# Modulation blocks of a two-layer hybrid trunk: two per filler among the heads, four moved to the branch projections

## The chip, the cores and the metric

The kernel runs on one core of a Trainium2 chip, as one launch. The metric is the device time of one execution in microseconds. The core has engines with instruction streams of their own: TensorE (PE; its weight loads are PEld) multiplies, VectorE (DVE) and ScalarE (ACT) do elementwise work, GpSimd (POOL) some rare steps, and SyncE (SP) issues most of the DMA loads. Each engine runs its row in order; semaphores join the rows.

## The reference

Two layers (L0, L1) work on one sequence of 256 positions with 1024 channels, in float32. A conditioning vector `c` gives each layer six modulation vectors of 1024 channels: shift, scale and gate for the mixer (1) and for the feed-forward part (2).

```
c_act = silu(c)
for l in range(2):
    mod = c_act @ ada_w[l] + ada_b[l]                 # 6 x 1024
    sh1, sc1, g1, sh2, sc2, g2 = split(mod, 6)
    h = rmsnorm(x) * (1 + sc1) + sh1
    x = x + g1 * mixer(h)
    h = rmsnorm(x) * (1 + sc2) + sh2
    x = x + g2 * conv_ffn(h)
return rmsnorm(x)
```

The mixer projects `h` once and feeds two branches of eight heads each: an attention with low-rank q and kv (block-causal softmax), and an mLSTM (weights `exp` of gate differences times `q k`, a normaliser, a head norm). Then `merged = sigmoid(g_mla) * (y_mla @ w_br_mla) + sigmoid(g_mlstm) * (y_mlstm @ w_br_mlstm)`, and `merged @ w_out`.

## The kernel before

Activations lie with their channels on the 128 partitions, as eight blocks of 128 channels by 256 positions. Every float32 matmul is done as three products of rounded parts, `fm_steps`: weight high part by activation high part, high by low, low by high. The class `_Weights` loads each weight tile `raw` (128x1024, 512 KB, seven buffers) on SP's queue; ScalarE copies it to the rounded high part `whi` (five buffers) and VectorE subtracts to get the low part `wlo` (four buffers). The matmuls of a weight tile cannot run before both.

The order of the work is written out as units. A `unit` (L265) is a list of slots, each a group of TensorE matmuls (12 in a slot of what follows). Ahead of each slot it calls `advance()`, by which all side generators (evictions, heads, merges) issue their next step, then it issues one piece of the weight splitting, then, where the slot's number is in `ada`, one `pump()`, and then the slot's matmuls.

`pump` (L344) takes the next modulation block from `background` and issues `ada_block` (L337): a DMA of 512 KB on SP's queue into one of two `wada` buffers, and one VectorE `scalar_tensor_tensor` over 128x1024 that multiplies by `silu(c)` and sums each row into one column of `mod`. After the eighth block of a modulation vector a tiny addition of the bias follows (and a halving for g1). The order in `background` is g1, sc2, sh2, g2 of the layer, eight blocks each, and in layer 0 then the first vectors of layer 1. Blocks of g1 are needed where `x` is updated by the output projection; sc2 and sh2 (blocks 9 to 24) at `norm_columns` (L1109), behind the branch projections, where `while (l, 3) not in done: pump()` would pump what is missing.

Among the heads the units are fillers: `run_filler(i)` (L813) is one weight tile of the gate or value projections, four slots, and the two generators of a head (`mla_head` L839, `mlstm_head` L885) advance by one step at each slot. So an attention head's steps (scores, maxima, `exp`, `reciprocal` and scaling, transposes on TensorE, copy, product with v) lie between the slots. `fill()` (L1051) runs the ten late fillers 0, 1, 4 to 11: one ahead of the heads, one after each head but 1 and 3, and the rest behind the last. Behind them come the eight units of the branch projections, of two slots each: for each half `c` of the columns two of the attention branch (`merge_a`, into `ua`) and two of the mLSTM branch (`merge_b`, which ends in the merged high part `mh` on ScalarE and low part `ml` on VectorE). Then the output projection, in which layer 0 pumps five blocks (`OUT_PUMPS`) and layer 1 none.

VectorE, ScalarE and GpSimd instructions may be moved by the scheduler, but not ahead of the one issued eight (two on GpSimd) before on the same engine; and a block's instruction stays behind the VectorE instruction issued last before it. Both layers run the same code.

Of the kernel before, what the change touches and what calls it, by code (L numbers as in the profile page):

```python
# [57 lines left out]

FILLERS_3 = (4, 5, 6, 7)
OUT_PUMPS = ((1, 2, 3, 4, 5), ())
UP_PUMPS = ((4, 6, 8), ())
DOWN_PUMPS = ((2, 2, 2, 2, 2, 1, 1, 1, 1, 1, 1), (1,) * 8)
# [128 lines left out]
def hybrid_trunk(ctx, tc, a):  # L193
# [26 lines left out]
    def bank():  # L220
        return psum.tile([P, 512], F32, name=nm("bank"), tag="bank", bufs=8)
# [16 lines left out]
    def v2(t):  # L238
        return t.rearrange("p (n t) -> p n t", n=2)
# [6 lines left out]
    def spawn(g):  # L246
        sides.append(g)
# [6 lines left out]
    def advance():  # L254
        for g in list(sides):
            try:
                next(g)
            except StopIteration:
                sides.remove(g)
# [5 lines left out]
    def unit(slots, evict=None, ada=()):  # L265
        for i, s in enumerate(slots):
            advance()
            W.emit_piece()
            if i in ada:
                pump()  # L270
            s()
        if evict is not None:
            spawn(evict)


    def fm_steps(out, w, h, ks, msl, h0=0, start=True, stop=True):

        wh, wl = w
        hh, hl = h
        for i, k in enumerate(ks):  # L280
            first = start and i == 0
            last = stop and i == len(ks) - 1
            pe.matmul(out, wh.at(k, msl), hh[:, h0 + k, :], start=first, stop=False)
            pe.matmul(out, wh.at(k, msl), hl[:, h0 + k, :], start=False, stop=False)
            pe.matmul(out, wl.at(k, msl), hh[:, h0 + k, :], start=False, stop=last)
# [58 lines left out]
    def pump():  # L344

        if not background:
            return
        l, ci = background.pop(0)
        ada_block(l, ci, wada)
        s, n_ = ci // 8, 1 if ci // 8 == 5 else 8  # L350
        if n_ == 1 or ci % 8 == 7:
            cols = mod[l][:, ci + 1 - n_:ci + 1]
            o = _OFF["adab"] + ci + 1 - n_
            dve.tensor_tensor(cols, cols, pp[:, l, o:o + n_], ALU.add)
            done.add((l, s) if n_ == 8 else (l, s, ci % 8))
            if s == 2:
                dve.tensor_scalar(cols, cols, 0.5, None, ALU.mult)
# [247 lines left out]
    def mixer(l, n, begun):  # L605
# [199 lines left out]
        def vm_slots(w, b):  # L805
            def slot(tb, k0):
                def run():
                    tm_steps(b[:, tb * T:(tb + 1) * T], w, h, range(k0, k0 + 4), tb, slice(0, 256),
                             start=k0 == 0, stop=k0 == 4)
                return run  # L810
            return [slot(tb, k0) for tb in range(2) for k0 in (0, 4)]

        def run_filler(i, ada=()):  # L813
            w = W.take()
            b = bank()
            if i < 2:
                unit(vm_slots(w, b), vm_evict(i, b), ada)
                return
            def slot(j, k0):
                def run():  # L820
                    fm_steps(b[:, j * T:(j + 1) * T], w, h, range(k0, k0 + 4), slice(j * P, (j + 1) * P),
                             start=k0 == 0, stop=k0 == 4)
                return run
            unit([slot(j, k0) for j in range(2) for k0 in (0, 4)], gate_evict(i - 2, v2(b)), ada)

        def vm_evict(c, b):
            for tb in range(2):
                dve.tensor_tensor(vaug[:, tb, 4 * c:4 * c + 4, 0:64],
                                  b[:, tb * T:(tb + 1) * T].rearrange("p (h d) -> p h d", h=4),
                                  ealo[:, tb, 4 * c:4 * c + 4].unsqueeze(2).to_broadcast([P, 4, 64]),  # L830
                                  ALU.mult)
            yield

        def gate_evict(i, b):
            dst, o = ((tho, 2 * i) if i < 2 else (tg[0], 2 * i - 4) if i < 6 else (tg[1], 2 * i - 12))
            act.activation(dst[:, o:o + 2, :], b, AF.Tanh, scale=0.5)
            yield
# [160 lines left out]
        for c in range(2):  # L998
            w = W.take()
            for hp in range(2):  # L1000
                b = bank()

                def slot(j, b=b, w=w, hp=hp):
                    def run():
                        fm_steps(b[:, j * T:(j + 1) * T], w, (ch[0], cl[0]), range(3),
                                 slice((2 * hp + j) * P, (2 * hp + j + 1) * P))
                    return run
# [3 lines left out]
        for hp in range(2):  # L1011
            b = bank()
# [8 lines left out]
        for tb in range(2):  # L1021
            b = bank()
# [27 lines left out]

        def fill():  # L1051
            i = left.pop(0)
            run_filler(i, ada=(0, 1, 2) if i in FILLERS_3 else (0, 2))

        fill()
        heads = []
        yb = nb = None
        for hd in range(NH):
            if hd % 2 == 0:
                pair, spair = [], []  # L1060
            if hd % 4 == 0:
                yb = bank()
                nb = (bank(), bank())
            heads += [mlstm_head(hd, nb, spair), delayed(MLA_DELAY[hd % 2], mla_head(hd, yb, pair))]
            sides.extend(heads[-2:])
            if hd not in PLAIN_HEADS:
                fill()
        while left:
            fill()
# [12 lines left out]
        def merge_b(m0, b):  # L1082
# [4 lines left out]
            yield  # L1087
            dve.tensor_tensor(ml[:, m0:m0 + 2, :], v2(t), mh[:, m0:m0 + 2, :].bitcast(F32), ALU.subtract)

        ya = [(yah[:, 2 * i:2 * i + 2, :], yal[:, 2 * i:2 * i + 2, :]) for i in range(2)]  # L1090
        for c in range(2):
            for y, merge in ((ya, merge_a), (yl, merge_b)):
                w = W.take()
                for q in range(2):
                    b = bank()

                    def slot(j, b=b, w=w, q=q, y=y):
                        def run():
                            for i in range(2):
                                fm_steps(b[:, j * T:(j + 1) * T], w, y[i], range(2 * i, 2 * i + 2),  # L1100
                                         slice((2 * q + j) * P, (2 * q + j + 1) * P), h0=-2 * i,
                                         start=i == 0, stop=i == 1)
                        return run

                    unit([slot(0), slot(1)], merge(4 * c + 2 * q, b))
        while (l, 3) not in done:
            pump()
        n = norm_start()
# [164 lines left out]
    for i in FIRST:  # L1273
        b = bank()
        begun[i] = b[:, :T], b[:, T:2 * T], v2(b)
    normalised(slice(0, 1))
    for k in range(KB):
# [26 lines left out]
        for u, ui in enumerate(FIRST):  # L1304
            for j in range(2):
                c = u * 256 + j * P
                i, c = c // 1024, c % 1024
# [25 lines left out]
    for l in range(DEPTH):  # L1333
        background.extend((l, 8 * s + i) for s in (2, 4, 3, 5) for i in range(8))
        if l + 1 < DEPTH:
            background.extend((l + 1, 8 * s + i) for s in (1, 0) for i in range(8))
        n = mixer(l, n, ((hh, hl), begun) if l == 0 else None)
        with tc.tile_pool(name=f"fx{l}", bufs=1, reuse_waits="tile") as fx:
            n = ffn(l, fx, n)
# [132 lines left out]
```

## Time and profile before

| What | Value |
| --- | --- |
| three runs | 830.99, 831.08, 834.4 us; median 831.08 us |
| the profiled execution | 829.05 us; its span, from the first to the last instruction, 827.3 us |
| PE busy | 794.7 us, 96% of the span, mean granted clock 0.986 |
| DVE busy | 688.4 us, 83% |
| ACT busy | 502.0 us, 61% |
| modulation blocks pumped during the trunk | 96, 118.4 us of DVE |
| heads and their fillers | near 100 to 187 us (L0), 495 to 581 us (L1) |
| branch projections | 188 to 210 us, 582 to 604 us |
| output projection | 210 to 235 us, 604 to 627 us |

Times in the trace count from the span's start. TensorE's clock has two levels; a granted clock of 1.00 is 2.4 GHz and of 0.50 is 1.2 GHz. A busy share is a mean over the whole span; a stretch is judged by its own idle time and by what ended it.

### The profile page before, as it was taken

The page shows a single profiled execution, that of the slowest core. Times are in us where ns is not written, and L with a number is a line of the kernel's source. Part 1 is how long each engine was busy: PE and PEld are TensorE (multiplying, and loading weights), DVE is VectorE, ACT ScalarE, POOL GpSimd, SP SyncE. Part 2 cuts the span into 40 slices and gives each one's busy share as a digit, 9 for nine tenths or more (in the row PEclk, how much of TensorE's full clock was granted, in tenths as well). Part 3 has the DMA queues.
Part 4 walks back from the last instruction along what each step waited for, and adds up shares of the span by engine and source line. Part 5 has one row for each costly group of instructions (what it writes and reads, how often), then busy time and mean ns, then how long its engine had stood idle before and what let it go on. Part 6 is the DMA issues. An engine that isn't in the chain of part 4 may idle for free.

```text
span 827.3 us, 16719 instructions
## 1 busy us (share of the span) xinstructions
PE 794.7 (96%) x6452; PEld 777.5 (94%) x6452; DVE 688.4 (83%) x1241; ACT 502.0 (61%) x918; POOL 79.0 (10%) x98
## 2 busy tenths in 40 slices
PE   5998989999999999999999999899999999999995
PEld 4998888999999999999999999799999999999995
DVE  5957988888989998888968987898887998888752
ACT  5674747664558766653548674676455876665551
POOL 4700020100010000000111001110011000000010
PEclk9998999999999999999999999999999999999998
DMA  9984587787765775468985468878754566546841
GB/s 338 396 287 133 184 328 259 237 284 258 239 219 175 244 239 182 142 199 305 327 328 179 133 203 303 278 250 284 255 180 159 178 204 197 182 142 202 296 125 51
DMA packets 57072, 188.34 MB, mean 228 GB/s; under 512 B 6576, under 2 KB 8352, under 8 KB 56992
## 3 DMA queue, kind: packets, MB, share of 16 engines
q1 hardware_dynamic: 55520, 183.89, 66.4%
q10 hardware_dynamic: 864, 2.23, 0.8%
q0 software_dynamic: 608, 1.16, 0.6%
q8 instruction: 50, 0.82, 0.4%
q14 instruction: 30, 0.25, 0.1%
HBM read 185.07 MB, written 1.06 MB: 225 GB/s over the span
## 4 chain that ended last, share of the span: by engine, by line
PE 57%; DVE 8%; DMA 4%; issue 3%; ACT 1%; DVEq 0%; POOLq 0%; POOL 0%; ACTq 0%
PE bank L184 57%; DMA ada<-in_ada 4%; DVE wlo L184 3%; DVE ada L184 2%; DVE w L184 1%; DVE hl L184 1%; DVE ub L184 0%; DVE z L184 0%; ACT whi L184 0%; DVE x L184 0%; ACT w L184 0%; DVE ua L184 0%; ACT ua L184 0%; ACT rs L184 0%; ACT sq L184 0%
## 5 line engine op out<-in xcount | busy, mean ns | idle before, releaser
L184 DVE TENSOR_TENSOR wlo<-raw,whi 128x1024 fp32r<-128x1024 f32 (+3 forms) x276 | 305.4, 1113 | 30.0 <-PE bank L184 10.5
L184 ACT CAST whi<-raw 128x1024 fp32r<-128x1024 f32 (+3 forms) x276 | 261.1, 955 | 114.1 <-PE bank L184 78.6
L184 PE MATMUL bank<-hh,whi 128*128 128x256 f32 x974 | 278.8, 287 | 0.0
L184 PE MATMUL bank<-hh,wlo 128*128 128x256 f32 x975 | 273.9, 281 | 1.1 <-DVE wlo L184 1.1
L184 PE MATMUL bank<-hl,whi 128*128 128x256 f32 x975 | 274.3, 282 | 0.0
L184 PEld LDWEIGHTS bank<-hh,wlo 128*128 128x128 f32 x975 | 184.3, 189 | 1.5 <-DVE wlo L184 1.5
L184 PEld LDWEIGHTS bank<-hl,whi 128*128 128x128 f32 x975 | 184.6, 189 | 0.9 <-DVE hl L184 0.3
L184 PEld LDWEIGHTS bank<-hh,whi 128*128 128x128 f32 x974 | 184.3, 189 | 1.1 <-issue 0.2
L184 DVE SCALAR_TENSOR_TENSOR ada<-ada,sact 128x1024 f32<-128x1024 f32 x96 | 118.4, 1237 | 21.0 <-DMA ada<-in_ada 20.7
L184 DVE SCALAR_TENSOR_TENSOR z<-bank,pp,z 128x255 f32<-128x255 f32 (+2 forms) x208 | 95.2, 477 | 17.0 <-ACT z L184 14.7
L184 PE MATMUL bank<-gh,wlo 128*128 128x256 f32 x352 | 99.0, 281 | 1.1 <-DVE wlo L184 1.1
L184 PE MATMUL bank<-gl,whi 128*128 128x256 f32 x352 | 99.1, 281 | 0.0
L184 PE MATMUL bank<-gh,whi 128*128 128x256 f32 x352 | 98.9, 281 | 0.0
L184 PEld LDWEIGHTS bank<-gh,wlo 128*128 128x128 f32 x352 | 66.3, 188 | 1.3 <-DVE wlo L184 1.3
L184 PEld LDWEIGHTS bank<-gl,whi 128*128 128x128 f32 x352 | 66.3, 188 | 0.0
L184 PEld LDWEIGHTS bank<-gh,whi 128*128 128x128 f32 x352 | 66.3, 188 | 0.0
L184 PE MATMUL bank<-ub,whi 128*128 128x256 f32 (+1 forms) x256 | 59.2, 282 | 0.0
L184 ACT ACTIVATE z<-bank,pp 128x256 f32<-128x256 f32 x96 | 49.1, 558 | 9.6 <-PE bank L186 5.6
L184 ACT ACTIVATE w<-z 128x256 f32<-128x256 f32 x60 | 25.0, 416 | 38.8 <-DVE z L184 37.1
L186 PE MATMUL bank<-hh,whi 128*128 128x256 f32 x146 | 46.1, 316 | 0.0
L184 PEld LDWEIGHTS bank<-ub,whi 128*128 128x128 f32 x256 | 43.9, 189 | 0.0
L186 PE MATMUL bank<-hh,wlo 128*128 128x256 f32 x145 | 42.7, 294 | 0.0
(253 smaller groups left out, 1390.3 us busy)
## 6 DMA issues: line engine op xcount, KB each, us to landing
ada<-in_ada SPq DMA_DIRECT2D x96, 512.0 KB, 5.1
raw<-in_w_up SPq DMA_DIRECT2D x88, 512.0 KB, 4.5
raw<-in_w_in SPq DMA_DIRECT2D x64, 512.0 KB, 5.6
raw<-in_w_down SPq DMA_DIRECT2D x32, 384.0 KB, 4.4
raw<-in_w_down SPq DMA_DIRECT2D x32, 320.0 KB, 3.9
raw<-in_w_out SPq DMA_DIRECT2D x16, 512.0 KB, 5.2
raw<-in_w_first SPq DMA_DIRECT2D x8, 512.0 KB, 8.1
raw<-in_w_bra SPq DMA_DIRECT2D x8, 512.0 KB, 5.2
```

The costliest lines, as they stand in the source:

```text
L184: r = f(*args, **kw)
L186: r = f(*args, **kw)
```

## The change

In each layer the fillers 4 to 7 pump at slots 0 and 2 like the others, and no more at slot 1 too. Among the heads 20 blocks are pumped in place of 24 per layer. The other four go to the units 0, 2, 4 and 6 of the eight units of the branch projections, at their first slot. The number of blocks and their order are the same.

```diff
-FILLERS_3 = (4, 5, 6, 7)
+BRANCH_PUMPS = (0, 2, 4, 6)
 OUT_PUMPS = ((1, 2, 3, 4, 5), ())
...
         def fill():
             i = left.pop(0)
-            run_filler(i, ada=(0, 1, 2) if i in FILLERS_3 else (0, 2))
+            run_filler(i, ada=(0, 2))
...
+        half = 0
         ya = [(yah[:, 2 * i:2 * i + 2, :], yal[:, 2 * i:2 * i + 2, :]) for i in range(2)]
...
-                    unit([slot(0), slot(1)], merge(4 * c + 2 * q, b))
+                    unit([slot(0), slot(1)], merge(4 * c + 2 * q, b), ada=(0,) if half in BRANCH_PUMPS else ())
+                    half += 1
```

Place 1 is VectorE's row in layer 0 at the second head's attention steps, around filler 4. `ada` is a block of the modulation, `wlo` a weight's low part, RECIPROCAL the attention head's (`sm`), `w_263` (`w_262` after) an mLSTM head's product. Before:

```order
L184 SCALAR_TENSOR_TENSOR ada_1396,mod_84<-ada_1396,sact 128x1024
L184 TENSOR_TENSOR wlo_1418<-raw_1289,whi_1417 128x1024
L184 SCALAR_TENSOR_TENSOR ada_1421,mod_84<-ada_1421,sact 128x1024
L184 RECIPROCAL sm_1439<-sm_1414 128x2
L184 SCALAR_TENSOR_TENSOR w_263_1477<-bank_1386,w_258_1446 128x384
L184 MEMSET bank_1443 64x2x64
L184 TENSOR_REDUCE sm_1474<-bank_1443 128x1 x2
L184 SCALAR_TENSOR_TENSOR ada_1450,mod_84<-ada_1450,sact 128x1024
```

After, the same row of VectorE:

```order
L184 SCALAR_TENSOR_TENSOR ada_1396,mod_84<-ada_1396,sact 128x1024
L184 TENSOR_TENSOR wlo_1418<-raw_1289,whi_1417 128x1024
L184 RECIPROCAL sm_1436<-sm_1414 128x2
L184 SCALAR_TENSOR_TENSOR ada_1447,mod_84<-ada_1447,sact 128x1024
L184 SCALAR_TENSOR_TENSOR w_262_1474<-bank_1386,w_257_1443 128x384
L184 MEMSET bank_1440 64x2x64
L184 TENSOR_REDUCE sm_1471<-bank_1440 128x1 x2
L184 TENSOR_TENSOR wlo_1526<-raw_1367,whi_1525 128x1024
```

No block stands between the subtract and the reciprocal any more; the next block stands between the reciprocal and the product `w`. Layer 1 has the same rows with other numbers.

Place 2 is VectorE's row one filler later in layer 0 (filler 5); `w_297` is again an mLSTM head's product, and the additions on `mod` close a modulation vector. Before:

```order
L184 TENSOR_TENSOR wlo_1561<-raw_1369,whi_1560 128x1024
L184 TENSOR_TENSOR mod_84<-mod_84,pp 128x8
L184 SCALAR_TENSOR_TENSOR ada_1564,mod_84<-ada_1564,sact 128x1024
L184 TENSOR_SCALAR mod_84<-mod_84 128x8
L184 RECIPROCAL sm_1583<-sm_1557 128x2
L184 MEMSET bank_1591 64x2x64
L184 SCALAR_TENSOR_TENSOR ada_1598,mod_84<-ada_1598,sact 128x1024
L184 SCALAR_TENSOR_TENSOR w_297_1619<-bank_1387,w_291_1587 128x384
```

After:

```order
L184 RECIPROCAL sm_1575<-sm_1552 128x2
L184 SCALAR_TENSOR_TENSOR ada_1590,mod_84<-ada_1590,sact 128x1024
L184 TENSOR_TENSOR mod_84<-mod_84,pp 128x8
L184 TENSOR_SCALAR mod_84<-mod_84 128x8
L184 SCALAR_TENSOR_TENSOR w_295_1613<-bank_1387,w_289_1579 128x384
L184 SCALAR_TENSOR_TENSOR w_297_1619<-bank_1519,w_291_1586 128x384
L184 MEMSET bank_1583 64x2x64
```

One block stands here in place of two, and none directly ahead of the product `w_297`.

Place 3 is VectorE's row in layer 0 at the end of the branch projections' first half: `ua` is what `merge_a` writes, `w_443` (`w_441` after) the sum of `merge_b`, and `ml` the low part that the output projection reads. Before:

```order
L184 TENSOR_TENSOR wlo_2297<-raw_2217,whi_2296 128x1024
L184 TENSOR_TENSOR wlo_2313<-raw_2219,whi_2312 128x1024
L184 SCALAR_TENSOR_TENSOR ua_1207<-ua_1207,bank_2294 128x2x256
L184 TENSOR_TENSOR wlo_2361<-raw_2290,whi_2360 128x1024
L184 SCALAR_TENSOR_TENSOR ua_1207<-ua_1207,bank_2328 128x2x256
L184 TENSOR_TENSOR wlo_2377<-raw_2292,whi_2376 128x1024
L184 SCALAR_TENSOR_TENSOR w_443_2393<-tgl_1209,bank_2358 128x512
L184 TENSOR_TENSOR w_443_2393<-w_443_2393,ua_1207 128x512
L184 TENSOR_TENSOR ml_2289<-w_443_2393,mh_2288 128x2x256
```

After:

```order
L184 TENSOR_TENSOR wlo_2284<-raw_2205,whi_2283 128x1024
L184 SCALAR_TENSOR_TENSOR ada_2287,mod_84<-ada_2287,sact 128x1024
L184 TENSOR_TENSOR wlo_2303<-raw_2207,whi_2302 128x1024
L184 SCALAR_TENSOR_TENSOR ua_1207<-ua_1207,bank_2281 128x2x256
L184 TENSOR_TENSOR wlo_2351<-raw_2277,whi_2350 128x1024
L184 SCALAR_TENSOR_TENSOR ua_1207<-ua_1207,bank_2318 128x2x256
L184 SCALAR_TENSOR_TENSOR ada_2354,mod_84<-ada_2354,sact 128x1024
L184 TENSOR_TENSOR wlo_2370<-raw_2279,whi_2369 128x1024
L184 SCALAR_TENSOR_TENSOR w_441_2386<-tgl_1209,bank_2348 128x512
L184 TENSOR_TENSOR w_441_2386<-w_441_2386,ua_1207 128x512
L184 TENSOR_TENSOR wlo_2425<-raw_2344,whi_2424 128x1024
L184 TENSOR_TENSOR ml_2276<-w_441_2386,mh_2275 128x2x256
```

Two blocks stand among the subtracts and merges, and a subtract now stands ahead of `ml`. On SP's queue the loads of the four blocks of each layer stand among the raw loads of the branch and output projections instead of those of the head fillers. From the up-projection on, the order on all engines is the same as before.

## Rows read from the trace of the kernel before

**Rows 1.** Page: span, and busy time (share, instructions) of each engine.
```profile
span 827.3 us, 16719 instructions
...
PE 794.7 (96%) x6452; PEld 777.5 (94%) x6452; DVE 688.4 (83%) x1241; ACT 502.0 (61%) x918; POOL 79.0 (10%) x98
```

**Rows 2.** Blocks (tile ada): VectorE's idle ahead (us, times), and loads, issue to landing.
```profile
  DMA ada<-in_ada: 20.7, 21
...
DMA to landing us min/median/max: 3.4/5.1/9.9
```

**Rows 3.** Timeline of PE: start, us, line, operation, out<-in, count [idle before <-what ended it].
```profile
124.63 1.09 PE L186 MATMUL bank<-cst,w 128*128 128x128 f32 x3 [2.73 <-ACT w L184]
...
138.49 0.92 PE L186 MATMUL bank<-kall,qall 128*128 128x128 f32 x4 [1.35 <-DVE w L184]
...
410.47 0.38 PE L184 MATMUL bank<-gh,wlo 128*128 128x256 f32 x1 [1.12 <-DVE wlo L184]
...
520.24 1.09 PE L184 MATMUL bank<-cst,w 128*128 128x128 f32 x3 [2.70 <-ACT w L184]
```

**Rows 4.** Stretches: us, busy PE, PEld, DVE, ACT, POOL (instructions), granted clock, DMA share, GB/s.
```profile
60.00:66.00 6.00, 6.00 (x30) 5.78 (x29) 1.97 (x6) 3.39 (x6) 2.22 (x3) 0.50 0.84 236
...
124.60:128.00 3.40, 3.37 (x13) 2.98 (x14) 1.75 (x4) 2.62 (x7) 0.00 (x0) 0.51 0.90 313
...
138.50:142.00 3.50, 3.50 (x28) 2.98 (x29) 3.42 (x8) 2.87 (x8) 0.00 (x0) 1.00 0.70 218
...
409.00:413.00 4.00, 2.88 (x25) 2.68 (x24) 4.00 (x11) 3.08 (x7) 2.43 (x1) 1.00 0.79 273
...
520.50:523.90 3.40, 3.33 (x14) 3.08 (x14) 3.35 (x7) 2.33 (x7) 0.00 (x0) 0.50 0.82 237
```

**Rows 5.** Timelines of DVE and ACT, heads of layer 0 (columns as in rows 3).
```profile
120.61 1.78 DVE L184 TENSOR_TENSOR wlo<-raw,whi 128x1024 fp32r<-128x1024 f32 x1
122.32 1.74 DVE L184 SCALAR_TENSOR_TENSOR ada<-ada,sact 128x1024 f32<-128x1024 f32 x1
...
123.99 0.15 DVE L184 RECIPROCAL sm<-sm 128x2 f32<-128x2 f32 x1
...
136.73 1.23 DVE L184 SCALAR_TENSOR_TENSOR ada<-ada,sact 128x1024 f32<-128x1024 f32 x1 [1.43 <-DMA ada<-in_ada]
...
137.88 0.55 DVE L184 SCALAR_TENSOR_TENSOR w<-bank,w 128x384 f32<-128x384 f32 x1
...
124.17 0.80 ACT L184 ACTIVATE w<-w,sm 128x128 f32<-128x128 f32 x2 [1.93 <-DVE sm L184]
```

**Rows 6.** Timelines of DVE and ACT, heads of layer 1.
```profile
518.39 1.28 DVE L184 SCALAR_TENSOR_TENSOR ada<-ada,sact 128x1024 f32<-128x1024 f32 x1 [1.08 <-DMA ada<-in_ada]
...
519.60 0.15 DVE L184 RECIPROCAL sm<-sm 128x2 f32<-128x2 f32 x1
...
516.97 1.03 ACT L184 CAST whi<-raw 128x1024 fp32r<-128x1024 f32 x1
...
519.79 0.80 ACT L184 ACTIVATE w<-w,sm 128x128 f32<-128x128 f32 x2 [1.79 <-DVE sm L184]
```

**Rows 7.** Stretches (columns as in rows 4): branch projections L0, output projections L0, L1.
```profile
188.40:210.30 21.90, 21.90 (x187) 21.90 (x187) 17.89 (x24) 9.29 (x12) 0.00 (x0) 1.00 0.74 257
...
210.30:239.00 28.70, 27.86 (x228) 26.95 (x227) 28.62 (x47) 15.31 (x27) 4.74 (x6) 1.00 0.78 253
...
604.30:632.60 28.30, 28.28 (x237) 27.93 (x237) 21.46 (x32) 15.53 (x27) 6.71 (x7) 1.00 0.59 188
```

**Rows 8.** Timelines of DVE and PE, layer 0, branch and output projections.
```profile
184.58 1.22 DVE L184 SCALAR_TENSOR_TENSOR ada<-ada,sact 128x1024 f32<-128x1024 f32 x1 [0.25 <-DMA ada<-in_ada]
...
188.54 2.36 DVE L184 TENSOR_TENSOR wlo<-raw,whi 128x1024 fp32r<-128x1024 f32 x2
...
214.99 0.68 DVE L184 TENSOR_TENSOR ml<-w,mh 128x512 fp32r<-128x512 f32 x1
...
221.56 0.39 PE L184 MATMUL bank<-mh,wlo 128*128 128x256 f32 x1 [0.38 <-DVE wlo L184]
```

## The prediction, made before the change was run

> **What bounds the kernel now.** I read the page's engine totals first: TensorE is busy for 794.7 of 827.3 us [rows 1], so a change that moves work of another engine can pay only in the 32.6 us in which TensorE stands, and in stretches at a lower clock. I then looked for TensorE rows with idle time ahead of them. In the stretches that the diff touches there are three of weight, all among the heads: 2.73 us ahead of the transposes at 124.63 and 1.35 us at 138.49 in layer 0, and 2.70 us at 520.24 in layer 1 [rows 3]. The table of stretches then shows the clock. After the two long idles TensorE gets 0.51 and 0.50 of full speed, which is the 1.2 GHz level instead of 2.4, for 3.4 us each; after the idle of 1.35 us, and after one of 1.12 us elsewhere (the row at 410.47), it stays at 1.00 [rows 3, 4].
>
> Who is late? The long wait names an activation on ScalarE, the scaling of the softmax weights. That one waits for VectorE's tiny reciprocal, which itself needs nothing late: it stands in VectorE's row behind two long instructions, a subtract `wlo` of 1.78 us and the modulation block `ada` of 1.74 us, and starts at 123.99 [rows 5]. This block is the one that filler 4 pumps at its slot 1. The wait of 1.35 us has the same form one filler later: the product `w` of an mLSTM head at 137.88 stands behind a third block, which itself had stood 1.43 us for its DMA [rows 5]. In layer 1 the reciprocal at 519.60 stands behind a block that had stood 1.08 us for its DMA [rows 6]. All three blocks are slot-1 pumps of fillers 4 and 5.
>
> **The change part by part. Blocks taken from the heads (gain).** The fillers pump 20 blocks per layer in place of 24. After the change the reciprocal of place 1 follows the `wlo` directly, and at place 2 both products `w` precede the next block.
> - Layer 0, first stall: the reciprocal can start when the subtract ends, at 122.32 (where the block started) instead of 123.99: 1.67 us less. Of 2.73 us some 1.06 stay.
> - Layer 0, second stall: `w` no longer stands behind a block that waits for its load: 1.35 us less.
> - Layer 1: the subtract ends at 518.39 − 1.08 = 517.31, but ScalarE copies a `whi` from 516.97 for 1.03 us, until 518.00. So the scaling moves from 519.79 to 518.00 and not to 517.5 [rows 6]: 1.79 us less, and 0.91 stays.
> - Clock: idles of 1.06 and 0.91 us are shorter than the 1.35 and 1.12 after which the clock stayed full, so I take both falls as gone. At half clock 3.4 us do the work of 3.4 × 0.51 or 0.50 [rows 4]: gains 1.67 and 1.70 us.
>
> Sum of the gains: 1.67 + 1.35 + 1.67 + 1.79 + 1.70 = 8.18 us. The two blocks dropped in fillers 6 and 7 gain nothing: no TensorE idle of over 0.5 us stands there, since TensorE's own work hides them.
>
> **Blocks added to the branch projections (cost).** Four blocks take 1.15 us of VectorE each (from the block at 136.73 to the next start at 137.88 [rows 5]), together 4.6 us. In layer 0 TensorE is busy in the whole stretch of the branch projections, and VectorE is idle for 21.90 − 17.89 = 4.01 us of it [rows 7]; so the blocks fit but for 0.6 us, if they fall into the idle. Not all do. There are two block buffers. A block of the heads runs 184.58 to 185.80, and only then its buffer can take the load of the second moved block, which needs 5.1 us by the median [rows 2, 8]. So that block can start near 190.9. Its turn comes after the first of the two subtracts at 188.54, near 189.7 [rows 8], so VectorE stands some 1.1 us, with the next weight subtracts queued behind. I walked through VectorE's new row of place 3 with these durations: the next subtracts slip, later idle takes most of it back, and the last `ml` of the branch projections, which ended at 214.99 + 0.68 = 215.67 [rows 8], ends near 216.5. That is 0.9 us late. From 210.3 to 239.0 VectorE is busy for 28.62 of 28.70 us, and TensorE waits for it in small pieces, such as 0.38 us at 221.56 [rows 7, 8]. There is nothing to make the 0.9 us good, and I take it on the path in full. If the cover holds wholly, the cost is 0; if no idle is usable, it is the 4.6 us of work; I take 0.9, since it is nearest to 4.6 − 4.01 = 0.6 with a piece of the DMA wait. In layer 1 VectorE is idle for 28.30 − 21.46 = 6.84 us in the output projection [rows 7], where five blocks are pumped in layer 0 and none here: a lag of 0.9 us is made good there. I take 0, ends 0 and 0.9.
>
> **Loads.** Each pump moves its 512 KB load on SP's queue as well. The count is unchanged, the four pass from among the head fillers' raw loads to the branch and output projections' raw loads. In the branch stretch the DMA engines are 0.74 to 0.78 busy [rows 7], and a `raw` load has seven buffers ahead of its use. I cost that at nothing beyond the wait above; if the cover fails, TensorE waits for a `wlo`, as in the 1.12 us at 410.47 [rows 3]. The three other changes of order (activations of the heads a place earlier, the matmuls of the output projection in another order) have no wait of note to lift, and cost nothing.
>
> Here a rule speaks for the change's cover: the Trainium skill ("Trainium Kernel Development and Optimization", Best Practices) advises double buffering so that a transfer overlaps the computation; by it two block buffers would hide the load, the 0.9 us would shrink to about 0.4 and the time be 823.3. The trace does not agree: with two buffers VectorE stood 20.7 us for these loads in all [rows 2]. The sum goes without it.
>
> **Sum.** 8.18 − 0.9 = 7.28 us. The profiled execution took 829.05 us (span 827.3 and 1.75 us around it), so it would become 821.8. It lies 2.03 us under the median of the three runs, 831.08, of which two agree (830.99 and 831.08). The predicted time is for such runs, so the same 7.28 comes off the median: **823.8 us**.
>
> **Rivals.**
> - *The clock still falls.* The stalls shorten as above, but the small head matmuls with idles of about 1 us left are too thin, and the clock falls all the same. For it: from 60 to 66 us the clock stands at 0.50 with TensorE busy in all 6.00 us [rows 4], so a fall doesn't need a long idle right ahead of it. Against: the idles of 1.35 and 1.12 us. It gives back 1.67 + 1.70 = 3.37 us: 827.2 us, a gain of 0.47%. The Trainium skill ("TensorE: Matmul & The Clock Gate", A second HAM failure mode: psum-queue depth-cycling) tells of frequent short gaps between groups of matmuls that make the clock swing and cost throughput; by it this rival would hold, and the row of 60 to 66 us agrees, the two of 1.00 behind idles don't.
> - *The wait is only handed on.* The next block now stands right behind the reciprocal and ahead of `w` (place 1), and in layer 1 its load would have to be there at about 517.4 while the load used at 518.39 came only then. Loads take up to 9.9 us [rows 2]. If a late load holds that block, both long stalls move on to `w` behind it and the clock falls with them; what is left is the second stall of layer 0, 1.35 us, against the cost of 0.9: a gain of 0.45 us, 830.6. For it: 20.7 us of VectorE's idle is for these loads. Against: with fewer blocks each buffer has longer to be filled.
> - *Slower: the blocks in the branch units reach TensorE.* Each unit ends in `merge` and a subtract on VectorE, and the weight subtracts stand in the same row. If the late blocks hold up the chain into `mh` and `ml` at the output projection's start, no idle of VectorE being usable, each layer pays 4.6 + 1.1 us, and 1.7 us for the clock fall that would follow an idle of this length: 7.4 us per layer, 14.8 against 8.18, so 837.7 us. It decides from the point at which TensorE stands for 2.7 us ahead of the output projection; below that it only eats part of the gain. Against: TensorE shows no idle in 21.90 us there, with `wlo` buffers ahead, and VectorE has 4.01 us.
> - *The change doesn't do what it says.* The instructions do move, so this would be that the slot-1 blocks were not the last cause (the scaling waits for something else as late). Its time is that of the handed-on wait, and it is counted with it.
>
> **How the numbers follow.** Forecast 823.8 with a chance of 0.61; clock still falls, 827.2, 0.20; handed on, 830.6, 0.12; slower, 837.7, 0.07. A measurement of this kernel can tell 0.5% from no change, 4.2 us: faster below 826.9, slower above 835.2. The forecast's own spread is 821.5 (a cost of 0, 822.9, and 1.4 of the 1.97 us of idle that I let stand) to 827.5 (the upper end of the cost, 4.6 us), with nearly all of it under 826.9. Faster by over 0.5%: the forecast's 0.61, and 0.07 of the second case where one fall of the two goes: 0.68. Within 0.5%: the rest of the second case and the third, 0.25. Slower: 0.07. The range must leave out no more than 0.2: from 821.5 to 829.5 it holds the forecast and the case of the clock, and leaves out the handed-on wait and the slower case, 0.19.
>
> **What would show it.** In the profile after: the rows ahead of the head transposes with idles near 1 us in place of 2.7, and the stretches behind them at 1.00; `w` of filler 5 no longer behind a DMA wait; VectorE near 4.6 us busier in the branch stretch of both layers, TensorE still without an idle of over 1 us there; in layer 0's output projection TensorE waiting for VectorE 0.9 us more in sum, in layer 1 none. Wrong would make me: a clock of 0.5 in either head stretch, an idle of over 2 us ahead of `w`'s matmuls, or an idle that ends with `mh`, `ml` or `wlo` at the start of the output projection.

## The result and the profile after

The first four runs of the changed kernel gave 820.51 us median (819.67 to 822.11), those of the kernel before 831.04 us: ratio 0.9896, 95% interval [0.9865, 0.9928]. A second pairing, with ten runs, gave 823.61 against 828.59 us, ratio 0.993 [0.9896, 0.9963]. So the change makes the kernel faster: by 0.7% and 1.0% in the two pairings, by 0.4% to 1.35% with their intervals. The forecast was 7.28 us, 0.88%.

The page of the first profiled execution: span, busy time (share, instructions) of each engine, and the group of the modulation blocks (busy, mean ns | idle ahead).

```profile
span 818.3 us, 16722 instructions
PE 788.9 (96%) x6452; PEld 772.6 (94%) x6452; DVE 689.9 (84%) x1241; ACT 501.1 (61%) x918; POOL 80.0 (10%) x98
...
L184 DVE SCALAR_TENSOR_TENSOR ada<-ada,sact 128x1024 f32<-128x1024 f32 x96 | 118.7, 1240 | 15.8 <-DMA ada<-in_ada 15.4
```

Against [rows 1] PE has the same instructions in 5.8 us less busy time and 3.2 us less idle time. Of the 5.8 us, 3.1 lie among the heads, where two stretches at half clock are gone, and 2.4 ahead of them. VectorE waits 15.4 us for block loads, 20.7 before [rows 2].

PE's timeline at the stalls (columns as in [rows 3]): layer 0's heads, layer 1's heads, the output projections.

```profile
120.67 0.84 PE L186 MATMUL bank<-cst,w 128*128 128x128 f32 x3 [0.84 <-ACT w L184]
121.85 0.92 PE L186 MATMUL bank<-kall,qall 128*128 128x128 f32 x4 [0.33 <-DVE w L184]
...
513.14 0.92 PE L184 MATMUL bank<-kall,qall 128*128 128x128 f32 x4 [1.02 <-DVE w L184]
...
209.00 0.50 PE L184 MATMUL bank<-mh,whi 128*128 128x256 f32 x2 [0.56 <-ACT mh L184]
215.90 0.39 PE L184 MATMUL bank<-mh,wlo 128*128 128x256 f32 x1 [0.85 <-DVE wlo L184]
...
600.47 0.50 PE L184 MATMUL bank<-mh,whi 128*128 128x256 f32 x2 [0.53 <-ACT mh L184]
```

The 2.73 and 2.70 us of [rows 3] have become 0.84 + 0.33 and 1.02 us, the 1.35 us at filler 5 are gone. New are idles in both output projections: for `mh` 5.5 us behind the projection's first matmul (which starts at 203.45 and at 594.93), and in layer 0 0.85 us for a `wlo`, where 0.38 us stood before [rows 8].

VectorE at place 1, layer 0, then layer 1:

```profile
118.42 1.22 DVE L184 TENSOR_TENSOR wlo<-raw,whi 128x1024 fp32r<-128x1024 f32 x1
119.56 0.16 DVE L184 RECIPROCAL sm<-sm 128x2 f32<-128x2 f32 x1
119.63 1.68 DVE L184 SCALAR_TENSOR_TENSOR ada<-ada,sact 128x1024 f32<-128x1024 f32 x1
...
121.25 0.55 DVE L184 SCALAR_TENSOR_TENSOR w<-bank,w 128x384 f32<-128x384 f32 x1
...
510.15 0.15 DVE L184 RECIPROCAL sm<-sm 128x2 f32<-128x2 f32 x1
510.93 1.68 DVE L184 SCALAR_TENSOR_TENSOR ada<-ada,sact 128x1024 f32<-128x1024 f32 x1 [0.62 <-DMA ada<-in_ada]
...
512.54 0.55 DVE L184 SCALAR_TENSOR_TENSOR w<-bank,w 128x384 f32<-128x384 f32 x1
```

The reciprocal follows the subtract at once, where it stood behind a block in [rows 5, 6]. The next block now stands ahead of `w`, and in layer 1 waits 0.62 us for its load: a small part of the wait was handed on.

Stretches (columns as in [rows 4]). Layer 0: behind the stall, the branch projections, the same from the first moved block on, the output projection. Layer 1: behind the stall, the branch projections from the first moved block on, the output projection up to the wait for `mh` and from there on.

```profile
122.60:126.00 3.40, 3.40 (x30) 3.16 (x29) 3.38 (x8) 1.79 (x6) 0.00 (x0) 1.00 0.98 366
...
180.80:203.40 22.60, 22.60 (x194) 22.60 (x193) 21.10 (x31) 9.22 (x11) 0.00 (x0) 1.00 0.86 304
183.97:203.40 19.43, 19.43 (x167) 19.43 (x166) 19.39 (x28) 7.68 (x9) 0.00 (x0) 1.00 0.86 306
...
203.50:232.20 28.70, 27.06 (x223) 26.25 (x222) 28.66 (x47) 15.89 (x28) 5.02 (x6) 1.00 0.85 275
...
514.00:518.00 4.00, 4.00 (x36) 3.77 (x35) 3.98 (x9) 2.05 (x8) 0.00 (x0) 1.00 0.80 263
...
575.40:594.90 19.50, 19.50 (x167) 19.50 (x166) 19.42 (x29) 7.70 (x9) 0.00 (x0) 1.00 0.85 299
595.00:600.40 5.40, 4.94 (x42) 4.74 (x40) 5.40 (x7) 2.67 (x6) 0.00 (x0) 1.00 0.90 301
...
600.40:623.30 22.90, 22.83 (x192) 22.79 (x193) 16.93 (x27) 13.40 (x24) 6.58 (x7) 1.00 0.62 197
```

The clock stays at 1.00 behind both stalls. From the first moved block on VectorE has no idle left through the end of the branch projections (19.39 of 19.43 us are busy in layer 0, 19.42 of 19.50 in layer 1); before, 17.89 of 21.90 us were used [rows 7].

To place the time, I took the starts of the same matmuls in every trace and formed the length of each stage, in us: all that lies ahead of the heads; heads with their fillers; branch with output projection; and the time from the heads of layer 0 to the end of the last feed-forward matmuls of layer 1. The last columns name the half-clock stretches in the heads, and the ratio of runs to the kernel before with its interval.

| kernel | ahead | heads L0 | branch+out L0 | heads L1 | branch+out L1 | sum from heads | half clock in heads | ratio |
| --- | --- | --- | --- | --- | --- | --- | --- | --- |
| before | 101.50 | 82.61 | 51.47 | 83.99 | 51.14 | 712.11 | L0, L1 | 1 |
| before_again | 102.12 | 83.10 | 51.47 | 83.21 | 51.18 | 712.64 | L0, L1 | 0.9992 [0.9959, 1.0025] |
| after | 99.43 | 77.94 | 52.08 | 80.85 | 51.56 | 705.27 | none | 0.9896 [0.9865, 0.9928] |
| after_again | 99.14 | 80.92 | 52.57 | 80.70 | 51.83 | 708.85 | L0 | 0.9930 [0.9896, 0.9963] |
| heads_only | 101.79 | 84.24 | 51.46 | 86.93 | 51.19 | 715.99 | L0 twice, L1 | 1.0007 [0.9979, 1.0036] |
| branch_only | 100.15 | 82.17 | 51.59 | 84.00 | 51.03 | 711.22 | L0 | 0.9996 [0.9975, 1.0017] |
| only_45 | 97.48 | 79.28 | 51.52 | 80.41 | 51.06 | 704.79 | none | 0.9935 [0.9910, 0.9959] |
| only_67 | 100.47 | 82.69 | 52.07 | 82.76 | 51.04 | 710.51 | L0 | 0.9987 [0.9965, 1.0008] |
| slot3 | 97.71 | 80.39 | 51.46 | 82.20 | 51.19 | 707.83 | none | 0.9953 [0.9925, 0.9981] |
| clump | 97.83 | 78.23 | 56.98 | 81.17 | 55.21 | 714.08 | none | 1.0020 [0.9992, 1.0047] |
| early_branch | 98.52 | 79.52 | 53.66 | 81.39 | 51.78 | 709.58 | none | 0.9898 [0.9861, 0.9935] |
| one_in_4 | 99.83 | 77.29 | 52.27 | 80.62 | 51.42 | 704.44 | none | 0.9877 [0.9842, 0.9911] |
| f4_03 | 102.00 | 78.60 | 51.53 | 79.15 | 51.08 | 703.33 | none | 0.9887 [0.9851, 0.9923] |
| f4_03_again | 102.38 | 78.95 | 52.98 | 80.48 | 51.02 | 707.18 | none | 0.9908 [0.9879, 0.9938] |

In the first pair of profiles the span fell by 9.0 us, but 2.07 of that lies ahead of the heads, where all engines have the same instructions in the same order. From the heads on the change gave 6.84 us: 4.67 and 3.14 gained in the heads, 0.61 and 0.42 lost behind them, and 0.07 elsewhere.

### The profile page after: what moved, and what is told of

Same layout as the page of the kernel before. It is cut to its first block, busy times and chain, and to the rows that moved or that the text cites. A ratio compares the mean times of both kernels' runs of the same rounds, so it can differ in the third digit from the quotient of the medians.

```text
span 818.3 us, 16722 instructions
## 1 busy us (share of the span) xinstructions
PE 788.9 (96%) x6452; PEld 772.6 (94%) x6452; DVE 689.9 (84%) x1241; ACT 501.1 (61%) x918; POOL 80.0 (10%) x98
## 3 DMA queue, kind: packets, MB, share of 16 engines
HBM read 185.07 MB, written 1.06 MB: 227 GB/s over the span
## 5 line engine op out<-in xcount | busy, mean ns | idle before, releaser
L184 DVE SCALAR_TENSOR_TENSOR ada<-ada,sact 128x1024 f32<-128x1024 f32 x96 | 118.7, 1240 | 15.8 <-DMA ada<-in_ada 15.4
```

Source lines behind the costliest of these rows:

```text
L184: r = f(*args, **kw)
```

## Experiments

**The two kernels again.** No edit.

> The changed kernel once more, against the kernel before on the same chip. Theory: from the heads on it is 6.8 us ahead in the trace (4.7 and 3.1 gained in the heads of the two layers, 0.65 and 0.41 lost behind); what lay ahead of the heads in the first pair of profiles (2.1 us) is the clock of the first 100 us, which differs from execution to execution of the same code. So the ratio of the medians should come near 0.992 (6.8 of 829), not the 0.987 of the first medians. Rival (the first 100 us are faster by the change): again 2 us less before the heads, 0.989 or under.

The ratio 0.993 fits. But the rival's sign came too: ahead of the heads the trace has 99.14 us, against 101.50 and 102.12 us in those of the kernel before. The three programs that were traced twice (before, after, f4_03) repeat this part to 0.6 us or better, so whether it goes with the program or with the execution isn't settled. The heads of layer 1 repeat (80.70); those of layer 0 don't: 80.92. PE's timeline and the stretch behind it show why.

```profile
118.46 0.89 PE L186 MATMUL bank<-kall,qall 128*128 128x128 f32 x4 [1.11 <-DVE vaug L184]
121.64 0.83 PE L186 MATMUL bank<-cst,w 128*128 128x128 f32 x3 [0.88 <-ACT w L184]
122.93 1.35 PE L186 MATMUL bank<-kall,qall 128*128 128x128 f32 x4 [0.46 <-DVE w L184]
```
```profile
123.40:126.60 3.20, 3.20 (x15) 3.02 (x14) 3.19 (x7) 1.35 (x5) 0.00 (x0) 0.50 0.99 296
```

The idles are 2.45 us in sum in place of 1.17, and the clock falls although the longest is 1.11 us. Idle (1.28) and clock (1.70) together are the 2.98 us between the two traces of the same program. Of the idle, 1.11 us is a wait for `vaug` that the first trace lacks. Such a wait, of 0.9 to 1.4 us, stands there in five of the 14 traces (before_again, after_again, only_45, early_branch, f4_03_again); what brings it is not shown.

> The kernel before once more, for a second trace. Theory: the idles ahead of the transposes come back in both layers at 2 to 3 us, since they hang on the order of VectorE's row; their size moves by some tenths with the loads of the blocks, and the clock of the first 100 us differs. Rival (the first trace caught an unlucky execution): an idle under 1.5 us in one of the layers, and then a smaller real gain.

PE's stalls of before_again, layer 0 and layer 1:

```profile
125.81 1.07 PE L186 MATMUL bank<-cst,w 128*128 128x128 f32 x3 [2.14 <-ACT w L184]
...
521.18 0.83 PE L184 MATMUL bank<-cst,w 128*128 128x128 f32 x3 [1.86 <-ACT w L184]
```

The long idles came back, smaller (with a new 1.08 us for `vaug` at 121.37), and with both clock falls; the heads took 83.10 and 83.21 us. The first trace was no unlucky execution.

**Which dropped blocks matter.** Two blocks per layer move instead of four, to units 0 and 4 (`BRANCH_PUMPS = (0, 4)`); only_67 has (4, 5) where only_45 has (6, 7):

```diff
-            run_filler(i, ada=(0, 2))
+            run_filler(i, ada=(0, 1, 2) if i in (6, 7) else (0, 2))
```

> Only fillers 4 and 5 lose their slot-1 block; 6 and 7 keep three; two blocks per layer move to the branch projections (units 0 and 4). Theory: all of the heads' gain (7.8 us in the trace from the heads on) and at most half of the cost of 1.1 us: 7.3 us under before. Rival (each dropped block is worth the same): half of the gain, 4 us under before.

> Only fillers 6 and 7 lose their slot-1 block; 4 and 5 keep three; two blocks per layer move to the branch projections (units 0 and 4). Theory: nothing is gained in the heads, both stalls of 2.7 us and their clock falls stay, and up to 0.5 us of cost behind: within 1 us of before. Rival (each dropped block is worth the same): 4 us under before.

With fillers 4 and 5 alone the heads gain 6.9 us, the cost behind is gone (51.52 and 51.06), and so the whole gain is there (7.3 us from the heads on by the trace, ratio 0.9935). With 6 and 7 alone the heads of layer 0 stay at 82.69 us, and the long stall stands there, now 3.15 us, with its clock fall; the ratio's interval holds 1.

```profile
124.31 1.09 PE L186 MATMUL bank<-cst,w 128*128 128x128 f32 x3 [3.15 <-ACT w L184]
```

In layer 1 that trace has 1.18 and 1.58 us of idle and no fall, 82.76 us: the size of the stall moves with the loads (the block ahead of the reciprocal waited 1.33 us for its load where the stall is 3.15 us, and not at all where it is 1.18).

**The place or the number.** slot3 is the kernel before with the extra block of fillers 4 to 7 at slot 3 in place of slot 1 (`ada=(0, 2, 3)`); heads_only is the kernel before with the extra blocks in other fillers:

```diff
-FILLERS_3 = (4, 5, 6, 7)
+FILLERS_3 = (6, 7, 8, 9)
```

> Kernel before, but the extra block of fillers 4 to 7 is pumped at slot 3 instead of slot 1: same blocks in the same filler, another place in VectorE's row; nothing in the branch projections. Theory (place): the reciprocals of place 1 in both layers no longer stand behind the extra block; first stalls fall from 2.7 to about 1 us, one or both clock falls go: 3 to 5 us under before. Rival (number of blocks per filler): the stalls return or move to the next head's step, within 1 us of before.

> Fillers 4 and 5 lose their slot-1 block, fillers 8 and 9 get it instead (3 blocks in fillers 6 to 9); nothing is pumped in the branch projections. Theory of the two stalls: the whole gain of the heads without the cost behind them: the clock falls at 2.7 us of idle are gone in both layers, 4.7 us less in layer 0 and 3.1 in layer 1, no DVE lag at the output projection; 7.8 us under the kernel before, some 1 us under the changed one in the stretch from the heads to the up-projection. Rival (the number of blocks among the heads matters, not the place): 24 blocks stay there, so nothing is gained, within 1 us of before.

slot3 did as the theory says: 0.74 us ahead of the transposes in layer 0, 0.52 in layer 1, no fall, ratio 0.9953, with as many blocks per filler as before. That is 4.3 us from the heads on, in place of the changed kernel's 6.8. heads_only refutes the assumption that other fillers hide a third block. The old stalls shrank (to 0.75 and 1.00 us in layer 0, where the clock still fell behind them, and 0.89 and 1.01 us in layer 1), and a new one opened in each layer at filler 8, with the clock behind it. PE, VectorE and a stretch of heads_only, layer 0:

```profile
170.94 0.33 PE L186 MATMUL bank<-cst,w 128*128 128x128 f32 x1 [1.61 <-ACT w L184]
```
```profile
165.59 1.23 DVE L184 SCALAR_TENSOR_TENSOR ada<-ada,sact 128x1024 f32<-128x1024 f32 x1 [2.09 <-DMA ada<-in_ada]
...
168.71 1.22 DVE L184 SCALAR_TENSOR_TENSOR ada<-ada,sact 128x1024 f32<-128x1024 f32 x1
169.85 0.08 DVE L184 DVE_READ_ACCUMULATOR ada<-ada,sact 128x1 f32 x1
169.85 0.16 DVE L184 RECIPROCAL sm<-sm 128x2 f32<-128x2 f32 x1
```
```profile
172.40:175.70 3.30, 3.30 (x18) 3.30 (x17) 2.22 (x7) 1.76 (x3) 1.64 (x1) 0.50 0.90 314
```

It is the same pattern in another place: a block that waited 2.09 us for its load, a second one, and behind them the reciprocal. The ratio alone (1.0007) is what the rival forecast; the trace shows where the new stalls stand, and slot3 that the same number of blocks can do with less.

**The cost behind the heads.** branch_only keeps three blocks in fillers 4 to 7 and takes the four from fillers 8 to 11; clump leaves `BRANCH_PUMPS` empty; early_branch uses units 0, 1, 2, 4.

```diff
-            run_filler(i, ada=(0, 2))
+            run_filler(i, ada=(0, 1, 2) if i in (4, 5, 6, 7) else (0,) if i in (8, 9, 10, 11) else (0, 2))
```
```diff
-BRANCH_PUMPS = (0, 2, 4, 6)
+BRANCH_PUMPS = ()
```
```diff
-BRANCH_PUMPS = (0, 2, 4, 6)
+BRANCH_PUMPS = (0, 1, 2, 4)
```

> Four blocks move to the branch projections as in the change, but they are taken from slot 2 of fillers 8 to 11; fillers 4 and 5 keep their three blocks. Theory: the two long stalls and the two clock falls of the kernel before stay (2.7 us each); the branch and output projections cost what they cost in the changed kernel, 0.65 us in layer 0 and 0.41 in layer 1: 1.1 us above the kernel before. Rival of full cover: 0. Rival that the branch units themselves bring a gain: several us under before.

> The change without its pumps in the branch units: the four blocks of each layer are pumped in a row behind the branch projections, ahead of the columns of the next norm. It measures what the cover of the branch units is worth. Theory (VectorE has no idle to take four blocks at once, and two buffers let two of the loads start only when a block is done): heads as in the changed kernel, but VectorE is late by 4.6 us of blocks and up to 5 us of load wait at the output projection, of which 3 to 7 us per layer reach TensorE, with a clock fall: 830 to 838 us. Rival (the output projection's idle takes it): under 825 us.

> The change with its four branch blocks at units 0, 1, 2 and 4 instead of 0, 2, 4 and 6: same number of blocks, none behind the last but two units. Theory (what costs is a block in the last merge chain, which makes mh and ml late at the start of the output projection): TensorE's time from the first matmul of the output projection on falls back from 29.4 to 29.9 us (layer 0) and 28.8 to 29.1 (layer 1) to the 28.8 and 28.4 of the kernel before; the heads as in the changed kernel; 0.5 to 1.4 us less than it. Rival (VectorE is short of time in sum, 4.6 us of blocks against its 4.0 us of idle): the output projection stays at 29.4 and 28.8 or more.

branch_only: no gain, as forecast, and no cost either, where I had expected 1.1 us (51.59 and 51.03 us, against 51.47 and 51.14): the same four blocks in the same units are free when the fillers ahead hold one block each. So the cost is not of the branch units alone. None of these four blocks waits for its load in either layer; in the changed kernel the first of the four waits 1.47 us in layer 0 and 0.57 us in layer 1. clump: in a row the four blocks cost 5.5 and 4.1 us, with idles of 0.99 and 2.01 us in layer 0's output projection and a clock fall (in layer 1 too):

```profile
211.20 0.39 PE L184 MATMUL bank<-mh,wlo 128*128 128x256 f32 x1 [0.99 <-DVE wlo L184]
214.65 0.58 PE L184 MATMUL bank<-mh,wlo 128*128 128x256 f32 x1 [2.01 <-DVE wlo L184]
```
```profile
214.10:220.80 6.70, 6.15 (x27) 5.89 (x28) 6.70 (x13) 1.48 (x3) 1.88 (x2) 0.50 0.92 304
```

That takes the whole gain. It is what the slower rival feared, by a `wlo` and not by `mh` or `ml`, at 5.5 and 4.1 us against the 7.4 per layer that I had put on it; the branch units keep it away. early_branch refutes my idea that the late block in the last merge is what costs: with no block there the output projection still waits 0.85 us for `mh`, and a first wait is added, since the early block waits longer for its load and the subtract behind it reaches TensorE:

```profile
185.68 1.23 DVE L184 SCALAR_TENSOR_TENSOR ada<-ada,sact 128x1024 f32<-128x1024 f32 x1 [2.37 <-DMA ada<-in_ada]
```
```profile
200.49 0.39 PE L184 MATMUL bank<-qm,wlo 128*128 128x256 f32 x1 [0.68 <-DVE wlo L184]
210.71 0.51 PE L184 MATMUL bank<-mh,whi 128*128 128x256 f32 x2 [0.85 <-ACT mh L184]
```

The cost goes with the number of moved blocks and with the wait of the first of them for its load. In layer 0, two cost 0.05 us where that wait was 2.02 us (only_45), 0.6 where it was 2.68 (only_67) and 1.5 where it was 3.65 (f4_03_again, below); three cost 0.8 at 2.35 (one_in_4); four cost 0.6 at 1.47 and 1.1 at 2.45 (the changed kernel twice). In layer 1, two cost nothing, three 0.3, four 0.4 and 0.7. No run changed the wait alone. The first moved block of only_67, then of f4_03_again:

```profile
190.65 1.23 DVE L184 SCALAR_TENSOR_TENSOR ada<-ada,sact 128x1024 f32<-128x1024 f32 x1 [2.68 <-DMA ada<-in_ada]
```
```profile
189.75 1.23 DVE L184 SCALAR_TENSOR_TENSOR ada<-ada,sact 128x1024 f32<-128x1024 f32 x1 [3.65 <-DMA ada<-in_ada]
```

**Better than both?** Two kernels also free the product `w` at place 1. one_in_4 (branch units 0, 2, 4) and f4_03 (units 0, 4):

```diff
+            run_filler(i, ada=(0,) if i == 4 else (0, 1, 2) if i in (6, 7) else (0, 2))
```
```diff
+            run_filler(i, ada=(0, 3) if i == 4 else (0, 1, 2) if i in (6, 7) else (0, 2))
```

> Filler 4 pumps one block (slot 0), filler 5 two, 6 and 7 three, and three blocks go to branch units 0, 2 and 4. Theory (place): the block between the reciprocal and the product w at place 1 is gone too, so the idles of 0.3 to 1.0 us ahead of the matmuls behind w go in both layers: heads of 77.5 to 79 and 80 us, the output projections at 28.8 and 28.4 with the last unit free: 8 us under before, a ratio near 0.990. Rival (the wait is handed on to the next head's step): heads as with two blocks in filler 4, 79.3 and 80.4, and no better than the changed kernel.

> Filler 4 pumps at slots 0 and 3, filler 5 at 0 and 2, 6 and 7 three, and only two blocks go to the branch units (0 and 4). Theory: the product w at place 1 stands ahead of the block again, the idle ahead of its matmuls goes, and two blocks in the branch units cost nothing: heads of 77.5 to 79 and 80 us, output projections 28.8 and 28.3; a ratio near 0.990. Rival (the block at slot 3 makes the maxima of the next head late): heads of 80.4 and 82.2 us as where all extra blocks stood at slot 3.

> The kernel with filler 4 at slots 0 and 3 and two branch blocks once more, for a second trace and a narrower interval. Theory: heads of 77 to 79 and 79 to 81 us and output projections of 28.8 and 28.3 again, whatever the clock of the first 100 us does; the ratio again at or under 0.990. Rival (its first trace was a lucky execution): a clock fall in one of the heads, 1.7 us more there, and a ratio near the changed kernel's 0.993.

In both the idle ahead of `w`'s matmuls is gone; 0.82 and 0.89 us ahead of layer 0's transposes stay. f4_03 has the least from the heads on (703.33) and costs nothing behind in its first trace; in its second layer 0's branch and output projections took 1.5 us more, with late `wlo` and `mh`. Ratios: 0.9877, 0.9887 and 0.9908. All lie under the kernel before; against the changed kernel's 0.9896 and 0.993 the intervals overlap, so a gain over it, some 2 us by the traces, is possible and not shown.

## Why the prediction was right

- **Which stalls, and why**: right. The blocks at slot 1 of fillers 4 and 5 made them (only_45), those of 6 and 7 had nothing to give (only_67), and the greater part hangs on their place in VectorE's row: slot3, with their number kept, has 4.3 of the 6.8 us. Whether the rest hangs on the number isn't separated.
- **Size in the heads**: layer 0 was to gain 1.67 + 1.35 + 1.67 = 4.69 us and gained 4.67 in the first pair; layer 1 was to gain 3.49 and gained 3.14. There 1.02 us of idle stayed in place of 0.91, now ahead of `w`: the handed-on rival held for 0.62 us of load wait; the other 0.24 us I can't place. The close fit in layer 0 is luck in part: after_again gains 1.7 us there.
- **The clock**: half right. I took idles of up to 1.35 us as harmless, from two rows. In the first trace both falls went; in after_again layer 0's came back with no idle over 1.11 us, and 1.70 us with it. So the rival "the clock still falls" is true of a part of the executions, and the gain from the heads on lies between about 7.1 and 3.5 us by the traces (712.4, the mean of before, against 705.27 and 708.85). The stretch from 60 to 66 us that I counted for small gaps has none: TensorE is busy in all 6.00 us of it [rows 4].
- **Cost in layer 0**: 0.9 us worked out, 0.61 and 1.10 measured. The load wait of the moved block was 1.1 us by my working; the trace has 1.47 us (the block at 183.97), at the first moved block and not the second: behind the block at 184.58 [rows 8] one more block of the heads follows, at 187.17, so the buffer it leaves is for the first moved one. VectorE's last `ml` was to be 0.9 us late and is 1.1 us late against the output projection's first matmul. TensorE waits 1.0 us more there (0.56 for `mh`, and 0.85 in place of 0.38 for the `wlo`), and 0.4 of it comes back at the stage's end.
- **Cost in layer 1**: the step that failed. I took 0, because VectorE has 6.84 us of idle in the output projection. But the idle comes behind the moment that matters. TensorE needs the second half's `mh` 5.5 us into that stage; up to there VectorE was busy before too (5.41 of 5.50 us), and nearly all its idle lies behind (16.05 of 22.80 us busy):

```profile
604.30:609.80 5.50, 5.48 (x46) 5.28 (x46) 5.41 (x8) 3.04 (x5) 0.00 (x0) 1.00 0.52 150
609.80:632.60 22.80, 22.80 (x193) 22.65 (x193) 16.05 (x24) 12.50 (x22) 6.71 (x7) 1.00 0.60 197
```

  After the change VectorE's sum `w` for this `mh` ends 1.1 us later against the stage's first matmul, TensorE waits 0.53 us for it (0.80 in after_again), and, busy in nearly all the rest, it can't win this back: the cost is 0.42 and 0.69 us. VectorE's idle later makes VectorE's lag good, not TensorE's.
- **The signs named beforehand**: two of those that were to prove a part wrong came, the idle for `mh` in the output projections and, in after_again, a clock of 0.50 in a head stretch. VectorE is busier by 2.5 us in layer 0's branch projections (21.10 us, against 18.59 in the same 22.60 us before), not by 4.6.
- **Median**: 823.8 forecast, 820.51 and 823.61 measured. The 820.51 lies 1 us under the range's low end; in the first pair of profiles 2.07 us come from ahead of the heads, where both kernels are the same (99.43 and 101.50 us), which I had no term for; whether the medians hold as much of it isn't shown. By ratios the forecast of 0.88% lies in both intervals.

VectorE's row for the first moved block, layer 0:

```profile
183.97 1.22 DVE L184 SCALAR_TENSOR_TENSOR ada<-ada,sact 128x1024 f32<-128x1024 f32 x1 [1.47 <-DMA ada<-in_ada]
```

## What to carry to other kernels

A long filler instruction on a shared engine costs by the instruction that stands right behind it: look for the tiny one (here a reciprocal of 0.15 us) on which TensorE waits, and move the filler past it, before moving it to another stage. Idle time of a helper engine can take moved work only if it lies ahead of the point where the bounding engine needs the result. And test the new place with what stands ahead of it: the same four blocks per layer were free behind thin fillers, cost 1.0 and 1.8 us behind full ones, and 9.6 us in a row.

## What the runs showed of the hardware

The first 100 us of identical code took 97.48 to 102.38 us over 14 traces, mostly by TensorE's clock. Between 50 us and the heads it stands at the 1.2 GHz level for 3.4 us in the three traces of 97.5 to 97.8 us, for 6.8 us in the six of 98.5 to 100.5, for 10.2 us in the two of 101.5 and 101.8, and for 13.6 us in the three of 102.0 to 102.4. The same stretch is at 1.2 GHz in one trace and at 2.4 in another, with the same single idle of 0.57 us some 2 us ahead of it in both. Stretches of before_again, then of only_45:

```profile
58.10:64.70 6.60, 6.60 (x33) 6.60 (x32) 2.30 (x6) 4.12 (x8) 2.22 (x3) 0.50 0.80 232
```
```profile
58.10:64.70 6.60, 6.60 (x57) 6.42 (x57) 5.05 (x11) 4.97 (x10) 2.23 (x3) 1.00 0.81 231
```

The same 30 matmuls take 6.40 us in the first and 3.49 in the second, so this one stretch moves an execution by some 3 us, nearly half of this change's gain; medians of the kernel before went from 827.98 to 831.04 us between sessions, and the granted clock of its single runs from 0.974 to 0.993. Nor does the length of an idle alone tell whether the clock falls: one of 2.45 us in branch_only, layer 1, was followed by 1.00, and the idles of 1.11, 0.88 and 0.46 us in after_again by 0.50, while 1.06, 0.88 and 0.39 us at the same place in only_45 were followed by 1.00. The rows of branch_only:

```profile
517.70 0.84 PE L184 MATMUL bank<-cst,w 128*128 128x128 f32 x3 [2.45 <-ACT w L184]
```
```profile
518.60:522.00 3.40, 3.40 (x30) 3.12 (x28) 3.38 (x8) 2.71 (x7) 0.00 (x0) 1.00 0.76 248
```

What decides between them these runs don't settle.
